# Sums of weight blocks made in DRAM by accumulating transfers, and loaded ready, in an encoder layer on one core

## Chip, cores and metric

The kernel runs on one core of a Trainium2 chip. The metric is the device time of one execution in microseconds. Three runs of the kernel before gave 1222.7, 1223.26 and 1224.56 us; the median is 1223.26 us.

## The reference

One layer of an encoder with 1024 tokens of width 1024, all in float32:

```python
h = rmsnorm(x, norm1_g) * (1.0 + sc1) + sh1
z = h @ w_in                                  # u, v, q, k, va, gate_a, gate_b
a_out = gmlp_branch(u, v, ...) @ w_a          # position mixing in chunks of 128, 8 groups
b_out = window_attention_branch(q, k, va, ...) @ w_b   # 8 heads, 2 kv heads, blocks of 128
merged = jax.nn.sigmoid(gate_a) * a_out + jax.nn.sigmoid(gate_b) * b_out
x = x + gt1 * (merged @ w_o)                  # w_o: 1024 x 1024

h2 = rmsnorm(x, norm2_g) * (1.0 + sc2) + sh2
f_gate, f_up = jnp.split(h2 @ w_ffn_in, 2, axis=-1)    # w_ffn_in: 1024 x 5632
x = x + gt2 * ((jax.nn.silu(f_gate) * f_up) @ w_ffn_out)
```

`sh1` to `gt2` come from a small conditioning product. The feed-forward has D_FF = 2816 hidden channels, 22 blocks of 128.

## The kernel before

**Products.** Each float32 operand is split into a high part (rounded by ScalarE) and a low part (the rest, by VectorE or GpSimd), and a product is three matmuls of 128x128 by 128x512. The gate products, the output projection and both feed-forward products are made by a scheme with seven block products in place of eight (Strassen's, in Winograd's form). It needs, besides blocks a11, a12, a21, a22 of a weight, sums and differences of them. In the kernel before, VectorE makes these sums from loaded weights: `merged_sums` (line 579) for w_o, in the attention stage of the second half of the tokens, with the result stored to the DRAM tile `sO`; `prep` (line 1812) for the gate and up weights of the feed-forward, block by block, into one tile `ws`, just before the split; `out_sums` (line 1911) for w_out, into the DRAM tile `wS`. The change touches the first two.

**Stages in order of time.** `half(0)` (line 643) handles the first 512 tokens: norm, the q/k product, the v product, eight attention steps (`for s in range(nw)`, line 1064), the spatial gating, the two branch projections. Then `half(1)` does the same for the other 512. `gate_products` (line 1385) makes the gate products for six column blocks d = 2 to 7, seven products each (i = 0 to 6). `out_products` (line 1489) is the output projection and the second norm. Then come 22 feed-forward blocks f, seven products each, and the second feed-forward product.

**An attention step.** At step s the scores of one block and kv head are made (`q_step`), the probabilities of the step before are transposed, exponentials are taken by ScalarE, `fill(FA)` and `fill(FB)` put three filler products (of u and of the gates) between them on TensorE, and `values` (line 552) multiplies by the values of the step before: ScalarE copies half of the result into a tile `xs` (a ring of two), VectorE adds, ScalarE makes the high part and GpSimd the low part (`mid<-xs,mid` in the profile). GpSimd also makes the low parts of filler weights (`prepare`, line 937; `wl<-raw,wh` on POOL) and the powers for the norms; after step 7 the one for `vr`, on which the spatial gating waits. In this stage the instructions of each compute engine are kept in program order.

**Queues.** Loads are issued by SyncE (SP), stores and a few loads by GpSimd, each in its own order. Weight units are loaded into a ring of three tiles `raw`; their high and low parts go to rings of three, `wh` and `wl`.

**Feed-forward order.** `order` (line 1991) lists the weight units (f, u), u = 1 to 3, in the order of preparation; `prepare(to, n)` (line 1998) makes up to n half preparations (high, then low) ahead of use. Unit 0 is the gate weight itself, units 1 and 2 are pairs of sums, unit 3 is a quarter of the up weight. In the kernel before, the gate weight of block f + 3 and the up weight of block f + 2 are loaded when units of block f are done.

Of the kernel before, what the change touches and what calls it, by code (L numbers as in the profile page):

```python
# [8 lines left out]
F32 = mybir.dt.float32  # L9
# [7 lines left out]
P = 128  # L17
# [90 lines left out]
def kernel(  # L108
# [58 lines left out]
    def nm(s):  # L167
        n_names[0] += 1
        return f"{s}_{n_names[0]}"
# [28 lines left out]
    def load(dst, src):  # L198
        ins = nc.sync.dma_start(dst, src)
        if not manual[0]:  # L200
            tc.keep_in_program_order(ins)

    def store(dst, src):
        nc.gpsimd.dma_start(dst, src)
# [112 lines left out]
    tA = dram.tile([NP, P, 4 * HALF], F32, tag="tA", name="tA")  # L317
    tB = dram.tile([NP, P, 4 * HALF], F32, tag="tB", name="tB")
    sO = dram.tile([KT // 2, P, 4 * HALF], F32, tag="sO", name="sO")


    apool_ctx = ExitStack()
# [66 lines left out]
    def ss_tile():  # L389
        return small.tile([P, 640], F32, tag="ss", name=nm("ss"), bufs=1)  # L390
# [182 lines left out]
    def open_ffn():  # L573
# [1 line left out]
        apool_ctx.close()  # L575
        fp = ffn_ctx.enter_context(pool("ffn"))
        fps.append(fp)

    def merged_sums(p):

        t = mid.tile([P, 2048], F32, tag="mid", name=nm("wo"))
        for i in range(2):
            load(t[:, i * UNIT : (i + 1) * UNIT], w_o[2 * p + i])
        a11, a12, a21, a22 = (t[:, i * HALF : (i + 1) * HALF] for i in range(4))
        ops = [(a22, a21, a22), (a21, a11, a21), (a11, a22, a11), (a12, a11, a12)]

        def one(n):
            out, a, b = ops[n]
            V.tensor_tensor(out, a, b, op=ALU.add)
            if n == 3:  # L590
                store(sO[p], t)
        return one

    halo_v = {}
    x1B = []
# [47 lines left out]
    def half(hf):  # L643
# [415 lines left out]
            V.tensor_copy(vgs[t], vps[t])  # L1059

        pts = None
        pair_sums = [merged_sums(0)] if hf else []
        adds = 0
        for s in range(nw):
            if s:
                prepare_due()
                sc = q_step(s)
                pts = transposed(st)
                den = exps(*sc, work[s][1])
            if hf == 0:  # L1070
                if s % 2 == 0:
                    ada_load()
                if s:
                    ada_late(*ada_loaded.pop(0), silu_c)
                if s == nw - 1:
                    ada_late(*ada_loaded.pop(0), silu_c)
            else:
                if s % 2 == 0 and s < nw - 2:
                    pair_sums.append(merged_sums(s // 2 + 1))
                for _ in range((0, 3, 3, 2, 2, 2, 2, 2)[s]):  # L1080
                    pair_sums[adds // 4](adds % 4)
                    adds += 1
            fill(FA)
            normalise(sc[0], sc[2], den)
            if s == 0:
                end_unit()
            st = sc[0]
            if s == nw - 1:
                for vg in vgs:
                    act[0] = after(A.activation(vg, vg, AF.Gelu_apprx_tanh), act[0])  # L1090
                for t, vg in enumerate(vgs[:3]):
                    V.tensor_tensor_reduce(
                        out=stream("hs"), in0=vg, in1=vg, op0=ALU.mult, op1=ALU.add,
                        scale=1.0, scalar=0.0, accum_out=vr[:, t : t + 1])
            if s:
                i, kv = work[s - 1]
                values(base + i, koff, kv, pts, vts, i, oH, oL)
            if s == nw - 1:
                A.activation(stream("hs"), vgs[3], AF.Square, accum_out=vr[:, 3:])
# [285 lines left out]
    def gate_products(hH, hL):  # L1385
# [21 lines left out]
        for d in GD:  # L1407
            banks = {}
            for i, (u, part, t, b, first) in enumerate(STEPS):
# [11 lines left out]
                elif i == 3:  # L1421
                    c22 = tmp()
                    A.copy(c22, bank)

                if i == 0:
                    gate_sums(d, 2)
                    gate_high(d, 2)
                elif i == 1:
                    gate_low(d, 2)
                elif i == 2:  # L1430
                    gate_high(d, 3)
                    merge(s, ps[1, 0])
                    gate_low(d, 3)
                elif i == 3:
                    gate_sums(d + 1, 1)
                elif i == 4:
                    gate_high(d + 1, 0)
                elif i == 5:
                    merge(c22, ps[0, 1])
                elif i == 6:  # L1440
                    gate_high(d + 1, 1)
                    merge(v, ps[0, 0])
                    V.tensor_tensor(merged[0][d // 4][:, d % 4, :], v, c22, op=ALU.add)
                    gate_low(d + 1, 1)
# [345 lines left out]
    T1, T2 = ((fpt(f"{n}h"), fpt(f"{n}l")) for n in ("tt1", "b22"))  # L1790


    RG, RU, U = {}, {}, {}
    a22 = []

    def gate_raw(f):
        r = wpool.tile([P, UNIT], F32, tag="raw", name=nm("raw"))
        dma(r, w_gate[f])
        return r

    def load_gate(f):
        if f < NF:
            RG[f] = gate_raw(f)
        else:
            fetch(f - NF)

    def load_up(f):
        if f < NF:
            RU[f] = ups[f % 2]
            dma(RU[f], w_up[f])  # L1810

    def prep(f, u, part):

        g, r = RG[f], RU.get(f)
        if part == 0:
            if u == 1:
                V.tensor_tensor(ws[:, Q:], r[:, :Q], r[:, Q:], op=ALU.add)
                V.scalar_tensor_tensor(out=ws[:, :Q], in0=ws[:, Q:], scalar=-1.0, in1=g[:, :Q],
                                       op0=ALU.mult, op1=ALU.subtract)
            elif u == 2:  # L1820
                V.tensor_tensor(ws[:, Q:], g[:, :Q], r[:, :Q], op=ALU.add)
                V.tensor_tensor(ws[:, :Q], g[:, Q:], ws[:, :Q], op=ALU.subtract)
            U[f, u] = wtiles(UNIT if u < 3 else Q)
            A.copy(U[f, u][0], (g, ws, ws, a22[0] if f == 0 else r[:, Q:])[u])
            return
        h, l = U[f, u]
        V.tensor_tensor(l, (g, ws, ws, a22[0] if f == 0 else r[:, Q:])[u], h.bitcast(F32), op=ALU.subtract)
        if u == 2:
            load_gate(f + 3)
        if u == 3 and f or (f, u) == (0, 2):  # L1830
            load_up(f + 2)

    BLK = {"B11": B11, "B21": B21, "T1": T1, "T2": T2}
    banks, keep, hidden = {}, {}, {}
# [94 lines left out]
    def low(src, t, k):  # L1929
        V.tensor_tensor(t[1][:, k, :], src, t[0][:, k, :].bitcast(F32), op=ALU.subtract)  # L1930
# [5 lines left out]
    def t2_sum(k):  # L1936
        V.scalar_tensor_tensor(out=X0[:, k, :], in0=X1[:, k, :], scalar=SHA(k + 4),
                               in1=X0[:, k, :], op0=ALU.add, op1=ALU.add)
        A.copy(T2[0][:, k, :], X0[:, k, :])

    def t34_sum(q, k):
        m = h2m[q][:, k, :]
# [12 lines left out]
    def chain_12(rb):  # L1955
        for k in range(4):
            chain.append(lambda k=k: scaled(X0, k, k, rb))
            chain.append(lambda k=k: t1_sum(k))
            chain.append(lambda k=k: scaled(X1, k, k + 4, rb))
            if k:  # L1960
                chain.append(lambda k=k: low(X0[:, k - 1, :], T2, k - 1))
            chain.append(lambda k=k: low(X0[:, k, :], T1, k))
            chain.append(lambda k=k: t2_sum(k))
        chain.append(lambda: low(X0[:, 3, :], T2, 3))

    def chain_rest():
        def new_block(name):
# [59 lines left out]
    def fetch(n):  # L2027
        if n < len(work):
            i, e = work[n]
            if outp:  # L2030
                r = outp[0].tile([P, UNIT], F32, tag="raw2", name=nm("raw2"))
            else:
                r = wpool.tile([P, UNIT], F32, tag="raw", name=nm("raw"))
            raws[n] = r
            dma(r[:, :Q], OUT[i][0](e))
            dma(r[:, Q:], OUT[i][1](e))
# [9 lines left out]

    with tc.manual_schedule():
        U[4, 0], U[5, 0], U[0, 0], U[1, 0] = early
        buf = mid.tile([P, 2048], F32, tag="mid", name=nm("ws"))
        ws, ups = buf[:, :UNIT], (buf[:, UNIT:], fp.tile([P, UNIT], F32, tag="ru", name="ru"))  # L2050
        load_up(0)
        load_up(1)
        g3 = gate_raw(3)
        load_gate(0)
        product(0, 0)
        U[2, 0] = wtiles()
        split2(raw2[0], *U[2, 0])
        evict(0, 0)
        load_gate(1)
        product(0, 1)  # L2060
        col_rstd(sums[1], NT, rcol[3])
        evict(0, 1)
        U[3, 0] = wtiles()
        split2(g3, *U[3, 0])
        load_gate(2)
        product(1, 0)
        rb = spread(rcol[3], NT)
        evict(1, 0)
        a22.append(ss_tile()[:, :Q])
        dma(a22[0], w_up[0][:, Q:])  # L2070
        prepare(0, 1)
        chain_12(rb)
        for f in range(1, EARLY):
# [246 lines left out]
```

## Time and profile before

| | |
|---|---|
| median of three runs | 1223.26 us (1222.7 to 1224.56) |
| profiled execution, its own time | 1221.94 us |
| its span, first to last instruction | 1220.2 us |
| granted TensorE clock, mean | 1.000 |
| TensorE (PE) busy | 1211.0 us, 99% of the span |
| VectorE (DVE) busy | 928.5 us, 76% |
| ScalarE (ACT) busy | 582.4 us, 48% |
| GpSimd (POOL) busy | 150.6 us, 12% |
| DMA packets | 236.54 MB, mean 194 GB/s |

A row of the timeline gives the start in us, the length in us, the engine and the operation with what it writes and reads; in brackets the engine's idle time before it and what ended that. A row of waits gives who waited, for whom, the total in us, the number of times and the longest. A row of a stretch gives its bounds, its length, busy times of PE, PEld (weight load), DVE, ACT and POOL, then the granted clock, the share of time in which the DMA engines were busy, and GB/s. L145 is the helper through which compute instructions are recorded, so the tiles tell them apart. DMA-issuing instructions are not counted as busy.

### The profile page before, as it was taken

What the parts mean: (1) busy time and instruction counts of PE and PEld (TensorE: products, weight loads), DVE (VectorE), ACT (ScalarE), POOL (GpSimd) and SP (SyncE); (2) the same over time, 40 slices, a digit from 0 to 9 for tenths busy, and PEclk for the clock granted to TensorE, in tenths of its full rate; (3) what the DMA queues carried; (4) which work ended last, traced back from release to release, by engine and by line L of the source; (5) the groups of instructions that cost most, each with busy time, mean ns of one, the idle gap of its engine ahead of it and who ended that gap; (6) DMA issues with size and microseconds to landing.
All of it is one profiled execution on the core that took longest, in us unless ns stands there. A gap on an engine that the chain in (4) does not pass through costs nothing.

```text
span 1220.2 us, 15626 instructions
## 1 busy us (share of the span) xinstructions
PE 1211.0 (99%) x5653; PEld 1007.2 (83%) x5653; DVE 928.5 (76%) x1504; ACT 582.4 (48%) x954; POOL 150.6 (12%) x182
## 2 busy tenths in 40 slices
PE   9999999999999999999999999999999999999998
PEld 7888888888888888877888888888888888888887
DVE  8999977789978776897997767675676766765646
ACT  5667865367855443644553333333333334433341
POOL 0024323024322000001100001000000000000001
PEclk9999999999999999999999999999999999999999
DMA  9752169653277233477313446455555449995552
GB/s 363 284 180 99 35 217 358 248 216 134 104 259 240 96 117 103 148 233 266 103 49 122 172 157 223 173 192 187 190 190 199 163 155 372 394 354 190 190 172 104
DMA packets 78096, 236.54 MB, mean 194 GB/s; under 512 B 8898, under 2 KB 9154, under 8 KB 72772
## 3 DMA queue, kind: packets, MB, share of 16 engines
q1 hardware_dynamic: 63028, 163.20, 38.6%
q0 software_dynamic: 14992, 72.36, 15.8%
q8 instruction: 44, 0.72, 0.3%
q14 instruction: 32, 0.26, 0.1%
HBM read 176.28 MB, written 59.24 MB: 193 GB/s over the span
## 4 chain that ended last, share of the span: by engine, by line
PE 93%; DVE 4%; issue 1%; DMA 1%; ACT 1%; POOL 0%; SPq 0%; DVEq 0%; ACTq 0%; POOLq 0%
PE mm L145 47%; PE at L145 46%; DVE mid L145 2%; DMA raw<-in_w_q_dram 1%; DVE wl L145 1%; DMA mid<-in_xA_dram 0%; DVE ss L145 0%; DVE h L145 0%; DVE ws L145 0%; ACT wh L145 0%; DVE t L145 0%; DVE tt1l L145 0%; ACT mid L145 0%; ACT h L145 0%; DVE b22l L145 0%
## 5 line engine op out<-in xcount | busy, mean ns | idle before, releaser
L145 DVE TENSOR_TENSOR wl<-raw,wh 128x1024 fp32r<-128x1024 f32 (+1 forms) x135 | 159.0, 1182 | 61.7 <-ACT wh L145 61.1
L145 ACT CAST wh<-raw 128x1024 fp32r<-128x1024 f32 (+1 forms) x149 | 152.2, 1023 | 112.1 <-PE mm L145 39.9
L145 PE MATMUL mm<-mid,wh 128*128 128x512 f32 x640 | 197.7, 390 | 0.8 <-DVE mid L145 0.8
L145 PEld LDWEIGHTS mm<-mid,wh 128*128 128x128 f32 x640 | 119.8, 188 | 25.8 <-DVE mid L145 1.2
L145 PE MATMUL mm<-wh,h 128*128 128x512 f32 x384 | 124.7, 397 | 0.5 <-ACT h L145 0.5
L145 PE MATMUL mm<-mid,wl 128*128 128x512 f32 x320 | 124.7, 390 | 0.0
L145 PE MATMUL mm<-h,wh 128*128 128x512 f32 x304 | 94.4, 392 | 0.0
L145 PE MATMUL at<-h,wh 128*128 128x512 f32 x304 | 93.9, 390 | 0.0
L145 PEld LDWEIGHTS mm<-wh,h 128*128 128x128 f32 x384 | 70.8, 188 | 14.2 <-ACT h L145 0.9
L145 DVE TENSOR_TENSOR wl<-ws,wh 128x1024 fp32r<-128x1024 f32 (+1 forms) x54 | 60.8, 1125 | 24.2 <-ACT wh L145 24.1
L145 ACT CAST wh<-ws 128x1024 fp32r<-128x1024 f32 (+1 forms) x54 | 52.5, 973 | 42.9 <-DVE ws L145 28.0
L145 PE MATMUL mm<-wl,h 128*128 128x512 f32 x192 | 71.2, 391 | 0.0
L145 PEld LDWEIGHTS mm<-mid,wl 128*128 128x128 f32 x320 | 60.1, 188 | 12.6
L145 PEld LDWEIGHTS at<-h,wh 128*128 128x128 f32 x304 | 56.9, 188 | 11.7
L145 PEld LDWEIGHTS mm<-h,wh 128*128 128x128 f32 x304 | 56.6, 188 | 11.6
L145 ACT ACTIVATE t<-t 128x512 f32<-128x512 f32 x46 | 28.4, 631 | 71.2 <-DVE t L145 71.2
L145 DVE TENSOR_TENSOR ol<-raw,oh 128x1024 fp32r<-128x1024 f32 x30 | 36.6, 1224 | 31.4 <-ACT oh L145 29.8
L145 PE MATMUL mm<-h,wl 128*128 128x512 f32 x152 | 59.4, 391 | 0.0
L145 PE MATMUL at<-h,wl 128*128 128x512 f32 x152 | 59.3, 390 | 0.0
L145 ACT ACTIVATE xs<-xs 128x512 f32<-128x512 f32 x21 | 13.3, 632 | 94.5 <-DVE xs L145 94.5
L145 ACT CAST oh<-raw 128x1024 fp32r<-128x1024 f32 x30 | 31.6, 1053 | 44.8 <-PE at L145 21.5
L145 PE MATMUL at<-wl,wh 128*128 128x512 f32 (+1 forms) x136 | 52.7, 388 | 0.0
(296 smaller groups left out, 2882.0 us busy)
## 6 DMA issues: line engine op xcount, KB each, us to landing
mid<-in_w_ada_dram SPq DMA_DIRECT2D x28, 512.0 KB, 8.3
raw<-in_w_gate_dram SPq DMA_DIRECT2D x28, 512.0 KB, 3.7
tA<-hid POOLq DMA_DIRECT2D x11, 1024.0 KB, 4.4
tB<-hid POOLq DMA_DIRECT2D x11, 1024.0 KB, 5.0
wo<-in_w_out_dram POOLq DMA_DIRECT2D x22, 512.0 KB, 5.9
wS<-wo POOLq DMA_DIRECT2D x11, 1024.0 KB, 5.2
raw<-wS SPq DMA_DIRECT2D x44, 256.0 KB, 3.4
raw<-tB SPq DMA_DIRECT2D x44, 256.0 KB, 5.2
```

The lines of the kernel that those rows point to most:

```text
L145: ins = f(*args, **kw)
```

## The change

The sums of w_o (all four pairs of blocks) and of the feed-forward's gate and up weights (all 22 blocks) are made in DRAM. For each group, four blocks of the weights are copied from DRAM to DRAM (to `sO`, or to a new DRAM tile `sF`) and four accumulating transfers add to them: two that need the copies, one that needs the first of these, one that needs the third. All are issued from GpSimd, each step behind a marker, a one-column copy on GpSimd that reads a tile of the compute stage, so that the step is issued at a chosen place. `plan_sums` gives the places: for w_o attention steps 0, 1, 3 and 5 of half 0; for feed-forward blocks 0 to 5 steps 1, 3, 5 and 7 of half 0; for blocks 6 to 11 steps 0, 2, 4 and 6 of half 1; for pairs of blocks from 12 to 21 products 0 and 4 of gate block d and of d + 1.

The feed-forward then loads units 1 and 2 ready from `sF` (two loads of 512 KB), and unit 3 as a quarter of the up weight (256 KB); each unit is loaded into a `raw` tile of its own, three units ahead. Two of the sums come with the opposite sign; the token block T2 is negated to match. `merged_sums` and the tiles of the sums on VectorE go.

```diff
+    sF = dram.tile([NF, P, 4 * HALF], F32, tag="sF", name="sF")
+
+    mark = [None]
+
+    def sum_dma(dst, src, **kw):
+        after(nc.gpsimd.dma_start(dst, src, **kw), mark[0])
+
+    def add_dma(dst, src):
+        sum_dma(dst, src, accum_op=ALU.add)
+
+    def sum_steps(dst, a11, a12, a21, a22):
+
+        S, w1, al, w2 = dst
+
+        def copies():
+            for d, a in zip(dst, (a11, a21, a12, a11)):
+                sum_dma(d, a)
+        return [copies, lambda: (add_dma(w1, a22), add_dma(w2, a21)), lambda: add_dma(S, w1),
+                lambda: add_dma(al, S)]
+
+    def quarters(t, f0, f1):
+        return [t[f0:f1, :, i * HALF : (i + 1) * HALF].rearrange("f p q -> p f q") for i in range(t.shape[2] // HALF)]
+
+    def ffn_sums(f0, f1):
+        return sum_steps(quarters(sF, f0, f1), *quarters(w_gate, f0, f1), *quarters(w_up, f0, f1))
+
+    def wo_sums():
+        w = [w_o.rearrange("(a b) p q -> b p a q", b=2)[i] for i in range(2)]
+        a = [w[i][:, :, j * HALF : (j + 1) * HALF] for i in range(2) for j in range(2)]
+        S, al, w2, w1 = quarters(sO, 0, KT // 2)
+        return sum_steps((S, w1, al, w2), *a)
+
+    sum_plan = {}
+
+    def plan_sums(steps, at):
+        for f, k in zip(steps, at):
+            sum_plan.setdefault(k, []).append(f)
+
+    def run_sums(ref, *k):
+        steps = sum_plan.pop(k, ())
+        if steps:
+            j = sm(8, "es")
+            mark[0] = G.tensor_copy(j[:, :1], ref)
+        for f in steps:
+            f()
+
+    plan_sums(wo_sums(), [(0, 0), (0, 1), (0, 3), (0, 5)])
+    plan_sums(ffn_sums(0, 6), [(0, 1), (0, 3), (0, 5), (0, 7)])
+    plan_sums(ffn_sums(6, 12), [(1, 0), (1, 2), (1, 4), (1, 6)])
+    for d in range(2, 7):
+        plan_sums(ffn_sums(8 + 2 * d, 10 + 2 * d), [(2, d, 0), (2, d, 4), (2, d + 1, 0), (2, d + 1, 4)])
...
-    def merged_sums(p):
...
@@ half(hf), attention steps
-            else:
-                if s % 2 == 0 and s < nw - 2:
-                    pair_sums.append(merged_sums(s // 2 + 1))
-                for _ in range((0, 3, 3, 2, 2, 2, 2, 2)[s]):
-                    pair_sums[adds // 4](adds % 4)
-                    adds += 1
+            run_sums(sc[1][:, :1], hf, s)
             fill(FA)
...
@@ gate_products
+                if i in (0, 4):
+                    run_sums((s if i == 0 else v)[:, :1], 2, d, i)
...
@@ feed-forward
+    def load_unit(n):
+        if n < len(order):
+            f, u = order[n]
+            if u == 0:
+                R[n] = gate_raw(f)
+            else:
+                R[n] = wpool.tile([P, UNIT], F32, tag="raw", name=nm("raw"))
+                if u < 3:
+                    dma(R[n], sF[f][:, (u - 1) * UNIT : u * UNIT])
+                else:
+                    dma(R[n][:, :Q], w_up[f][:, Q:])
         else:
-            fetch(f - NF)
+            fetch(n - len(order))
 
     def prep(f, u, part):
...
         if part == 0:
-            if u == 1:
-                V.tensor_tensor(ws[:, Q:], r[:, :Q], r[:, Q:], op=ALU.add)
-                V.scalar_tensor_tensor(out=ws[:, :Q], in0=ws[:, Q:], scalar=-1.0, in1=g[:, :Q],
-                                       op0=ALU.mult, op1=ALU.subtract)
-            elif u == 2:
-                V.tensor_tensor(ws[:, Q:], g[:, :Q], r[:, :Q], op=ALU.add)
-                V.tensor_tensor(ws[:, :Q], g[:, Q:], ws[:, :Q], op=ALU.subtract)
...
+            U[f, u] = wtiles(w.stop)
+            A.copy(U[f, u][0], R[n][:, w])
+        else:
+            split_low(R[n][:, w], *U[f, u])
+            load_unit(n + 3)
...
-        A.copy(T2[0][:, k, :], X0[:, k, :])
+        A.activation(T2[0][:, k, :], X0[:, k, :], AF.Identity, scale=-1.0)
+
+    def t2_low(k):
+        V.scalar_tensor_tensor(out=T2[1][:, k, :], in0=X0[:, k, :], scalar=-1.0,
+                               in1=T2[0][:, k, :].bitcast(F32), op0=ALU.mult, op1=ALU.subtract)
```

More of the change, by code (lines that the diff above doesn't have):

```diff
@@ L577, in open_ffn @@
         fps.append(fp)
-    def merged_sums(p):
[L581 to L592, printed above, removed]
     halo_v = {}
@@ L1061, in half @@
         pts = None
-        pair_sums = [merged_sums(0)] if hf else []
-        adds = 0
         for s in range(nw):
@@ L1790 @@
     T1, T2 = ((fpt(f"{n}h"), fpt(f"{n}l")) for n in ("tt1", "b22"))
-    RG, RU, U = {}, {}, {}
-    a22 = []
+    U, R = {}, {}
     def gate_raw(f):
@@ L1799, in gate_raw @@
         return r
-    def load_gate(f):
-        if f < NF:
-            RG[f] = gate_raw(f)
-        else:
-            fetch(f - NF)
[L1807 to L1810, printed above, removed]
+    def load_unit(n):
[9 more added lines that the diff above has]
+                    dma(R[n][:, :Q], w_up[f][:, Q:])
+        else:
+            fetch(n - len(order))
     def prep(f, u, part):
-        g, r = RG[f], RU.get(f)
+        n, w = place[f, u], slice(0, UNIT if u < 3 else Q)
         if part == 0:
-            if u == 1:
-                V.tensor_tensor(ws[:, Q:], r[:, :Q], r[:, Q:], op=ALU.add)
-                V.scalar_tensor_tensor(out=ws[:, :Q], in0=ws[:, Q:], scalar=-1.0, in1=g[:, :Q],
-                                       op0=ALU.mult, op1=ALU.subtract)
-            elif u == 2:
-                V.tensor_tensor(ws[:, Q:], g[:, :Q], r[:, :Q], op=ALU.add)
-                V.tensor_tensor(ws[:, :Q], g[:, Q:], ws[:, :Q], op=ALU.subtract)
[L1823 to L1831, printed above, removed]
+            U[f, u] = wtiles(w.stop)
[3 more added lines that the diff above has]
+            load_unit(n + 3)
     BLK = {"B11": B11, "B21": B21, "T1": T1, "T2": T2}
@@ L1960, in chain_12 @@
             if k:
-                chain.append(lambda k=k: low(X0[:, k - 1, :], T2, k - 1))
+                chain.append(lambda k=k: t2_low(k - 1))
             chain.append(lambda k=k: low(X0[:, k, :], T1, k))
             chain.append(lambda k=k: t2_sum(k))
-        chain.append(lambda: low(X0[:, 3, :], T2, 3))
+        chain.append(lambda: t2_low(3))
     def chain_rest():
@@ L2048 @@
         U[4, 0], U[5, 0], U[0, 0], U[1, 0] = early
[L2049 to L2052, printed above, removed]
         g3 = gate_raw(3)
-        load_gate(0)
+        load_unit(0)
         product(0, 0)
@@ L2058 @@
         evict(0, 0)
-        load_gate(1)
+        load_unit(1)
         product(0, 1)
@@ L2064 @@
         split2(g3, *U[3, 0])
-        load_gate(2)
+        load_unit(2)
         product(1, 0)
@@ L2068 @@
         evict(1, 0)
-        a22.append(ss_tile()[:, :Q])
-        dma(a22[0], w_up[0][:, Q:])
         prepare(0, 1)
```

## The prediction

> **What bounds the kernel now.** I read the page first, then the waits, then stretches of the timeline around the change.
>
> ```profile
> span 1220.2 us, 15626 instructions
> PE 1211.0 (99%) x5653; PEld 1007.2 (83%) x5653; DVE 928.5 (76%) x1504; ACT 582.4 (48%) x954; POOL 150.6 (12%) x182
> PE 93%; DVE 4%; issue 1%; DMA 1%; ACT 1%; POOL 0%; SPq 0%; DVEq 0%; ACTq 0%; POOLq 0%
> ```
>
> TensorE is busy for 1211.0 of 1220.2 us and carries 93% of the chain that ended last. All idle time of PE together is 9.2 us, a part of it at the start and the end, where this change does nothing. So work taken off VectorE pays only where PE stood waiting for VectorE, and everything else that the change does can only cost. The waits of PE and the stretches where VectorE is fullest say how much that is:
>
> ```profile
> PE mm L145 <- DVE mid L145: 0.8, 1, 0.8
> 263.00:295.00 32.00, 31.93 (x165) 26.46 (x164) 31.19 (x82) 21.86 (x57) 8.50 (x6) 1.00 0.43 158
> 598.00:617.00 19.00, 18.69 (x83) 15.18 (x83) 18.86 (x29) 9.75 (x16) 0.00 (x0) 1.00 0.21 79
> 264.60 0.16 DVE L145 TENSOR_TENSOR es<-rows,nmx 128x4 f32<-128x4 f32 x1
> 282.76 0.35 DVE L145 TENSOR_TENSOR es<-rows,nmx 128x4 f32<-128x4 f32 x1
> 291.54 0.55 DVE L145 TENSOR_TENSOR es<-rows,nmx 128x4 f32<-128x4 f32 x1
> 299.83 0.33 DVE L145 TENSOR_TENSOR es<-rows,nmx 128x4 f32<-128x4 f32 x1
> 316.42 0.35 DVE L145 TENSOR_TENSOR es<-rows,nmx 128x4 f32<-128x4 f32 x1
> ```
>
> A row of a stretch gives its length, then the busy time of PE, PEld, DVE, ACT and POOL, the granted clock, the DMA share and GB/s. In 263 to 295 us (attention steps of the second half, where the sums of w_o are made) VectorE is busy for 31.19 of 32 us. The `es` rows mark the steps: the fourth (282.76 to 291.54) takes 8.78 us, the next 8.29, so about 0.5 us is lost there. In 598 to 617 us (the feed-forward's first blocks) PE misses 0.31 us. The 0.8 us wait for `mid` is in the output projection, which keeps its VectorE work.
>
> **The sums on VectorE go.**
>
> ```profile
> L145 DVE TENSOR_TENSOR wo<-wo x60: 678/684/694, 274.2 to 1001.7; 128x512 f32<-128x512 f32 x60
> L145 DVE TENSOR_TENSOR ws<-raw,ws x33: 682/685/693, 607.0 to 990.5; 128x512 f32<-128x512 f32 x33
> ```
>
> 16 sums of w_o blocks (of the 60 `wo` rows; 44 are w_out's and stay) at 684 ns are 10.9 us; 22 x 4 sums of feed-forward blocks at 685 ns are 60.3 us. So 71 us leave VectorE, but PE gets back only the 0.5 + 0.3 = 0.8 us above. The sign change of T2 swaps operations of one shape for others: nothing. The loads and stores of w_o pairs go as well, 8.4 MB in the second half; the DMA shares that I use below still hold them.
>
> **The new loads of the feed-forward.**
>
> ```profile
> raw<-in_w_gate_dram SPq DMA_DIRECT2D x28, 512.0 KB, 3.7
> 391.37 2.72 PE at L145 x12
> ```
>
> A product of 12 matmuls takes 2.72 us (the chain's row), a block of seven 19 us. Per block f, 512 + 512 KB become 512 + 2 x 512 + 256 KB, 0.79 MB more, or 17.3 MB over 22 blocks, 419 us: 41 GB/s. A load lands in 3.7 us and is asked for three units ahead, about 14 us (four units in 19 us). I cost it at nothing; the cover is these 10 us of lead, and if it went, a load of 3.7 us would stand in front of a split once per unit. On SP's queue each load still waits only for its tile of three, as the gate weights' do now. The sums are first read near 600 us (the `ws` rows begin at 607.0) and are begun from 82 us on, so no load waits for a sum.
>
> **The transfers on GpSimd's queue.** Here is the cost. The diff issues copies and, behind them, additions that need the copies' landing. A DMA that needs another's landing holds GpSimd's queue, and the trace has this already:
>
> ```profile
> POOL wo L1257 <- DMA wS<-wo: 18.1, 4, 5.6
> L207 POOL DMA_DIRECT2D hd<-mid x1: 920/920/920, 48.9 to 48.9; - x1
> q0 software_dynamic: 14992, 72.36, 15.8%
> ```
>
> Behind the waiting addition stand GpSimd's own steps of the attention stage: the low parts of the outputs (`mid<-xs,mid`, 1.28 us), those of filler weights (`wl<-raw,wh`, 2.40) and the power of `vr`. Issuing one such DMA costs 0.92 us (512 rows), call it 1.
>
> Prices. GpSimd's queue moved 72.36 MB in 15.8% of 16 engines' 1220.2 us: 375 GB/s. A DRAM-to-DRAM transfer isn't in the trace. A copy costs between one move (375) and a load plus a store (188); I take one move, since the row counts a transfer's read and write once. An addition reads two blocks and writes one: between one move and three; I take two. So a w_o block set (1.05 MB) costs 2.8 us copied and 5.6 added, a set of six feed-forward blocks (1.57 MB) 4.2 and 8.4, times what other loads leave free:
>
> ```profile
> 82.00:106.00 24.00, 23.96 (x132) 20.27 (x131) 22.57 (x63) 16.34 (x44) 6.51 (x4) 1.00 0.45 161
> 106.00:122.00 16.00, 16.00 (x87) 13.78 (x86) 15.25 (x43) 11.88 (x30) 6.83 (x5) 1.00 0.20 67
> 122.00:146.00 24.00, 24.00 (x125) 19.98 (x124) 22.68 (x62) 20.16 (x48) 7.33 (x4) 1.00 0.15 45
> 81.90 0.16 DVE L145 TENSOR_TENSOR es<-rows,nmx 128x4 f32<-128x4 f32 x1
> 90.65 0.15 DVE L145 TENSOR_TENSOR es<-rows,nmx 128x4 f32<-128x4 f32 x1
> 106.32 0.55 DVE L145 TENSOR_TENSOR es<-rows,nmx 128x4 f32<-128x4 f32 x1
> 122.92 0.16 DVE L145 TENSOR_TENSOR es<-rows,nmx 128x4 f32<-128x4 f32 x1
> 111.12 1.28 POOL L145 TENSOR_TENSOR mid<-xs,mid 64x512 fp32r<-64x512 f32 x1 [4.27 <-ACT mid L145]
> 112.37 2.40 POOL L145 TENSOR_TENSOR wl<-raw,wh 128x1024 fp32r<-128x1024 f32 x1
> 125.67 0.59 ACT L145 COPY xs<-at 64x512 f32<-64x512 f32 x1
> 149.17 1.01 POOL L145 TENSOR_TENSOR vr<-vr,nhalf 128x4 f32<-128x4 f32 x1
> 154.65 1.21 DVE L145 TENSOR_TENSOR wl<-raw,wh 128x1024 fp32r<-128x1024 f32 x1
> 157.69 0.40 PE L145 MATMUL at<-mid,wh 128*128 128x256 f32 x2
> ```
>
> First half, by those rows. Step 0 (81.9): four w_o copies, 11.2 us at 55% free, land at 102. Step 1 (90.7): the w_o additions wait until 102; behind them 11.2 us of additions and 16.8 us of feed-forward copies, together 28.0: 2.1 by 106, 12.8 by 122, 13.1 at 85% free: 137.4. Step 3 (106.3): the feed-forward additions wait until 137.4. Two issues and the low part put the latter's end at 140.7 instead of 112.4. Its `xs` tile, one of two, is due again for ACT's copy at 125.67: PE loses 15.0 us, since VectorE and ACT stand behind that copy. Then 5.6 + 8.4 + 8.4 us of additions end at 144.0, 153.9 and 163.8. Step 5's sum waits for the second and issues at 154.9, its 8.4 us ending (behind w_o's last 5.6) at 180.3. Step 7's addition waits for that, and the power of `vr` starts at 182.6, due at 149.17 + 15.0 = 164.2; cover is 1.8 us (VectorE's last split ends at 155.86, PE needs it at 157.69): 16.6 lost. Half 0: 31.6 us. By one move per addition the same steps give 8.5 (all at the `xs` tile), by three 60, and 20 more in the second half.
>
> Second half: only feed-forward blocks 6 to 11.
>
> ```profile
> 295.00:311.00 16.00, 16.00 (x87) 13.79 (x86) 15.14 (x41) 13.07 (x33) 5.48 (x4) 1.00 0.26 98
> 311.00:327.00 16.00, 16.00 (x88) 13.38 (x87) 14.69 (x42) 12.88 (x32) 7.84 (x5) 1.00 0.31 113
> 302.51 0.58 ACT L145 COPY xs<-at 64x512 f32<-64x512 f32 x1 [1.05 <-PE at L145]
> 332.58 1.03 POOL L145 TENSOR_TENSOR vr<-vr,nhalf 128x4 f32<-128x4 f32 x1
> ```
>
> Copies: 16.8 us at 57% free from 264.6: 294. The wait of step 2 (282.76) ends there, the low part at 297.3, due at 302.51: nothing. The two additions end at 305.6 and 317.4, the third at 329.6; step 6 (316.42) waits for it, then four short steps, `vr` at 335.9 instead of 332.58: 1.5 us beyond the cover.
>
> Gate products, blocks 12 to 21:
>
> ```profile
> 407.69:483.85 76.16, 76.16 (x337) 63.09 (x337) 53.55 (x74) 30.99 (x45) 0.00 (x0) 1.00 0.33 105
> ```
>
> Each pair takes 5.6 + 11.2 us, five pairs 84 us at 67% free: 125 us from 391, done by 516. GpSimd has nothing else to do there (0.00 busy): no cost.
>
> Sum on the profiled execution's 1221.9 us: -0.8 + 31.6 + 1.5 = +32, 1254.2. The median shown is 1223.3, 1.3 above that execution: 1255.5, say 1256.
>
> **The rivals.** *Not slower: no waiting addition stands ahead of GpSimd's work.* If the waiting DMAs come out behind that work in its stream (the diff orders them only behind a marker), or land in time, the price is 0 and the gain 0.8: 1222.5. It decides at the low part of step 3: written before 125.67 or not. For it: the spacing of two steps (16.6 us) fits 6.3 MB at 375 GB/s on an idle queue. Against it: w_o has one step (9 us) for copies of 11.2, the loads take 15 to 45%, and the stage keeps GpSimd's steps in program order.
>
> *Far slower: a copy costs a load and a store, an addition three moves.* By the same steps at half and a third of 375 GB/s, step 1 waits until 117, step 3 until 177; the low part is 54 us late and `vr` 38 more; in the second half the copies land at 317, the low part 18 us late, `vr` 25 more: +135, 1357, and the lag could reach the output projection. The Trainium skill ("DMA: Bandwidth & Descriptors", "Latency and other measured facts") gives 207 to 214 GB/s for copies between HBM tensors; by it the 6.29 MB would take about 30 us instead of 16.8. No run here shows it. For this rival: both ends lie in one memory. Against: the one-move row is the only one of this queue.
>
> **How the numbers follow.** No blocking 0.24: 0.19 within 0.2% (2.4 us, about what the three runs, 1.9 us apart, can tell), and 0.05 faster, were VectorE's relief worth three times the 0.8. Forecast 0.46, with its own range from one move (1231) to three (1302) per addition. Far slower 0.30. The range goes from 1221 to 1320: some 0.04 lie below, some 0.15, the worse half of the far case, above. Slower: 0.76.
>
> **What would show it.** Right: GpSimd waits of 10 us and more for landings of the sums' transfers, ACT's `xs` copies late in steps 5 to 7, PE idle at 125 to 190 us, the second half nearly unhurt, VectorE 71 us emptier. Wrong: copies landing at other rates than 375 GB/s, PE busy through 80 to 160 us, or new waits for `raw` after 590 us.

## The result, and the profile after

The changed kernel takes 1260.68 us (median of 4 runs, 1259.23 to 1261.33) against 1222.98 for the kernel before in the same runs: a ratio of 1.031, 95% interval 1.0289 to 1.0326. The forecast was 1256 in 1221 to 1320. The profiled execution took 1260.43 us.

The page of the kernel after, the lines that answer to those of before (the last row is the granted TensorE clock in 40 slices):

```profile
span 1258.7 us, 15746 instructions
PE 1222.5 (97%) x5653; PEld 1016.3 (81%) x5653; DVE 877.1 (70%) x1400; ACT 579.0 (46%) x954; POOL 219.0 (17%) x263
PEclk9998879999999999999999999999999999999999
q0 software_dynamic: 35408, 122.70, 33.7%
PE 74%; DMA 16%; DVE 3%; issue 3%; ACT 2%; POOL 2%; SPq 0%; POOLq 0%; DVEq 0%; ACTq 0%
```

VectorE is 51 us emptier, not 71: the 104 sums are gone, but others of its instructions, most of them in half 0, take about 11 us longer (below). And busy time counts rows that overlap only once: the kernel of copies below, where nearly nothing is stretched, is 63 us emptier. PE still ends later: its idle time rises from 9.2 to 36.2 us, and its busy time by 11.5 us although it does the same 5653 matmuls. Transfers now carry 16% of the chain.

Both kernels have PE's matmuls in the same order, so the lag (the start of one and the same matmul, after minus before) tells where the time goes. In us, by stage, for the kernel after and for the experiments below (half 0 from 94 us on, ahead of the first hold):

| kernel | half 0 | half 1 | gate stage | output projection and first feed-forward blocks | rest |
|---|---|---|---|---|---|
| predicted | 31.6 | 1.5 | 0 | -0.8 (half 1's 0.5 included) | 0 |
| after | 28.2 | 0.4 | 12.5 | -2.6 | -0.4 |
| copies in place of additions | 0.3 | -1.3 | 1.8 | -2.7 | -0.4 |
| marker on its own column | 28.7 | 0.4 | 8.2 | -1.9 | -0.4 |
| holds without traffic | 19.0 | 0.0 | 1.0 | -0.4 | -0.2 |
| longer holds without traffic | 24.3 | -0.1 | 0.4 | 1.5 | 0.4 |
| other places, all blocks in DRAM | 1.0 | 1.1 | 0.8 | -2.7 | 24.3 |
| 6 blocks in DRAM | 1.0 | -1.2 | 0.7 | -2.4 | 2.3 |
| 12 blocks in DRAM | 0.7 | -1.3 | 0.2 | -2.3 | 1.2 |
| 16 blocks in DRAM | 0.9 | -1.2 | 11.4 | -2.7 | 1.2 |
| w_o early | 3.6 | -1.2 | 0.7 | -2.6 | 2.8 |
| needless addition at the scalings | 4.6 | 0.0 | 0.0 | 0.4 | -0.4 |
| the same behind the scalings | 0.0 | 0.0 | 0.7 | 1.1 | -0.5 |

Each row is one profiled execution. Where a kernel leaves a stage as it was, the lag still moves, by -0.4 to 1.5 us at the output projection.

Half 0 in the kernel after. First the timeline of GpSimd (brackets: idle time before, and what ended it), then the waits from 86 to 200 us (total, times, longest), then two stretches (PE, PEld, DVE, ACT, POOL busy, granted clock, DMA share, GB/s):

```profile
101.67 1.35 POOL L325 DMA_DIRECT2D sO<-in_w_o_dram  x1 [7.44 <-DMA sO<-in_w_o_dram]
136.84 1.38 POOL L325 DMA_DIRECT2D sF<-in_w_up_dram  x1 [9.11 <-DMA sF<-in_w_gate_dram]
137.68 1.83 POOL L145 TENSOR_TENSOR mid<-xs,mid 64x512 fp32r<-64x512 f32 x1
152.26 1.39 POOL L325 DMA_DIRECT2D sF<-sF  x1 [6.69 <-DMA sF<-in_w_up_dram]
175.12 1.38 POOL L325 DMA_DIRECT2D sF<-sF  x1 [12.06 <-DMA sF<-sF]
177.23 1.59 POOL L145 TENSOR_TENSOR vr<-vr,nhalf 128x4 f32<-128x4 f32 x1
...
PE at L145 <- DVE xs L145: 10.0, 2, 5.0
ACT mid L145 <- POOL vr L145: 8.0, 1, 8.0
ACT xs L145 <- POOL mid L145: 5.9, 1, 5.9
PE at L145 <- DVE lb L145: 5.0, 1, 5.0
...
90.00:120.00 30.00, 24.93 (x122) 20.88 (x122) 28.66 (x62) 17.48 (x44) 15.68 (x12) 0.91 1.06 316
120.00:150.00 30.00, 25.07 (x114) 21.31 (x113) 20.59 (x56) 17.88 (x45) 10.00 (x8) 0.86 1.07 276
```

The additions wait as forecast, and GpSimd's own steps stand behind them. But PE stops three times for about 5 us (near 112, 136 and 158 us) and once more behind `vr`, not twice; only one stop stands behind ScalarE's wait for the `xs` tile, the others behind VectorE. And the clock is granted at 0.86 to 0.91, where it was 1.00.

The gate stage, 420 to 550 us, the waits of the kernel after; behind them the landing of one group of loads from 440 to 545 us, first in the kernel before, then in the kernel after (last figure: median us from issue to landing):

```profile
DVE gsum L145 <- DMA raw<-in_w_gb_dram: 12.4, 4, 4.1
DVE t L145 <- POOL es L145: 8.3, 3, 4.5
DVE t L145 <- DMA xs<-pd: 6.7, 3, 2.6
PE mm L145 <- ACT t L145: 5.2, 2, 4.3
PE mm L145 <- DVE t L145: 3.6, 3, 1.6
...
raw<-in_w_gb_dram SPq DMA_DIRECT2D x2, 512.0 KB, 3.8
raw<-in_w_gb_dram SPq DMA_DIRECT2D x4, 512.0 KB, 10.1
```

Three new waits of VectorE stand here: for the marker (`es`, GpSimd's copy of a column of `s` or `v`, which VectorE then writes again), for gate weights that now land in 10.1 us, and for `xs` tiles loaded from the DRAM tile `pd` (256 KB each, stored there by the two halves). PE stops for 5.2 us behind ScalarE, which stands behind VectorE's wait for the marker, and for 3.6 us behind VectorE's `t`, which stands behind the loads. The forecast had none of them.

### The profile page after: what moved, and what is told of

It reads as the page before. It is cut to its first block, busy times and chain, and to the rows that moved or that the text cites. A ratio compares the mean times of both kernels' runs of the same rounds, so it can differ in the third digit from the quotient of the medians.

```text
span 1258.7 us, 15746 instructions
## 1 busy us (share of the span) xinstructions
PE 1222.5 (97%) x5653; PEld 1016.3 (81%) x5653; DVE 877.1 (70%) x1400; ACT 579.0 (46%) x954; POOL 219.0 (17%) x263
## 3 DMA queue, kind: packets, MB, share of 16 engines
q0 software_dynamic: 35408, 122.70, 33.7%
## 4 chain that ended last, share of the span: by engine, by line
PE 74%; DMA 16%; DVE 3%; issue 3%; ACT 2%; POOL 2%; SPq 0%; POOLq 0%; DVEq 0%; ACTq 0%
PE at L145 39%; PE mm L145 36%; DMA sF<-in_w_up_dram 8%; DMA sF<-sF 4%; DMA sO<-in_w_o_dram 1%; DVE mid L145 1%; DMA mid<-in_w_ada_dram 1%; POOL sF L325 1%; DMA raw<-in_w_q_dram 1%; DVE wl L145 1%; DMA raw<-in_w_ada_dram 1%; ACT mid L145 1%; DMA mid<-in_xA_dram 1%; ACT lb L145 0%; ACT wh L145 0%
## 5 line engine op out<-in xcount | busy, mean ns | idle before, releaser
L145 DVE TENSOR_TENSOR wl<-raw,wh 128x1024 fp32r<-128x1024 f32 (+1 forms) x201 | 227.8, 1136 | 129.6 <-ACT wh L145 128.9
L145 ACT CAST wh<-raw 128x1024 fp32r<-128x1024 f32 (+1 forms) x215 | 211.8, 987 | 113.3 <-PE at L145 38.3
L145 DVE TENSOR_TENSOR xs<-at,xs 128x512 f32<-128x512 f32 (+1 forms) x44 | 30.3, 689 | 37.9 <-PE at L145 30.5
L145 PE MATMUL at<-wh 128*128 128x512 f32 (+1 forms) x136 | 52.7, 387 | 0.0
L145 PE MATMUL at<-wh,wl 128*128 128x512 f32 (+1 forms) x136 | 52.7, 387 | 0.0
```

What stands on the lines that cost most here:

```text
L145: ins = f(*args, **kw)
```

## The experiments

**Traffic without holds.** Every transfer stays at its place with its size, but all eight are plain copies that wait for nothing.

```diff
-        return [copies, lambda: (add_dma(w1, a22), add_dma(w2, a21)), lambda: add_dma(S, w1),
-                lambda: add_dma(al, S)]
+        return [copies, lambda: (sum_dma(xw1, a22), sum_dma(xw2, a21)), lambda: sum_dma(xS, a21),
+                lambda: sum_dma(xal, a11)]
```

> All eight transfers of each group are issued at their old places, but as plain copies of input blocks to DRAM blocks of their own: same number of transfers and same sizes, no addition, no transfer that needs another's landing. The sums are left out, so the feed-forward and the output projection read other numbers. Theory (GpSimd's queue is held by additions that wait; what stands behind them is late): the lag against the kernel before at the end of half 0 falls from 28.4 us to 3 or less, the lag of the gate stage from 12.4 to 2 or less, the whole time is 1219 to 1229 us. Rival (the transfers' traffic itself slows loads and engines): copies move 2 bytes where additions move 3, so about three quarters of the traffic stays, and three quarters of the loss: 1247 to 1253 us. Rival (the traffic lowers TensorE's granted clock): granted clock stays near 0.9 from 90 to 180 us although PE does not stand idle, +8 to +12 us.

Measured: 1218.75 us, ratio 0.997 (0.9957 to 0.9983). One stretch of half 0, and the software queue's row:

```profile
120.00:150.00 30.00, 30.00 (x154) 24.88 (x153) 28.78 (x75) 25.39 (x59) 13.97 (x13) 1.00 1.02 343
q0 software_dynamic: 28752, 122.70, 29.1%
```

The DMA engines are full (1.02) here too, PE is busy without a gap, and the clock stays at 1.00. Both rivals fall for half 0. The row also prices the transfers: from 15.8% of 1220.2 us to 29.1% of 1216.9 is 161 us of all 16 engines, to 33.7% of 1258.7 is 231; with 11 us for the stores of w_o that went, 172 us for 54.5 MB as copies (317 GB/s) and 242 us where half of them are additions. So an addition costs (242 - 86) / 86 = 1.8 copies, by an estimate that takes copies to cost the same in both kernels.

**Holds without traffic.** The kernel before, with chains of tiny additions (2 KB) in half 0, each waiting for the one before.

```diff
+    HOLD = {0: 0, 1: 4, 3: 10, 5: 3, 7: 5}
...
+            for i in range(HOLD[s]):
+                after(nc.gpsimd.dma_start(hb[i % 2], hb[1 - i % 2], accum_op=ALU.add), m)
```

> The kernel before, with its sums on VectorE, and in half 0 at the same places chains of tiny accumulating transfers (2 KB each, 4, 10, 3 and 5 of them at steps 1, 3, 5 and 7), each needing the landing of the one before, so that GpSimd's queue is held for about 9, 22, 7 and 11 us while nearly no bytes move. Theory (holding alone): PE idles at the same steps, lag at the end of half 0 of 18 to 30 us, the whole time 1241 to 1253 us, and the granted clock falls to about 0.9 behind the idle stretches. Rival (traffic): lag of 3 us or less, 1223 to 1226 us, granted clock 1.0.

Measured: 1240.6 us, ratio 1.0141 (1.0124 to 1.0158). As these holds ended earlier than the sums' (step 1's low part starts at 100.07 us, in the kernel after at 105.89), a second run had longer chains: `HOLD = {0: 0, 1: 6, 3: 9, 5: 4, 7: 6}`.

> The kernel before with the chains of tiny additions made 6, 9, 4 and 6 long at steps 1, 3, 5 and 7, so that each holds GpSimd about as long as the sums do in the changed kernel (about 15, 22, 8 and 14 us from the marker on). Theory (holds and the catching up behind them are all of half 0's loss): lag at the end of half 0 of 24 to 31 us, 1246 to 1254 us. Rival (the transfers' traffic adds the 9 us by which the shorter chains fell short): lag of 22 us or less, 1240 to 1245 us.

Measured: 1246.4 us, ratio 1.0194 (1.0178 to 1.021). One stretch of the second kernel:

```profile
120.00:150.00 30.00, 25.79 (x126) 22.10 (x125) 21.25 (x60) 18.10 (x43) 15.36 (x17) 0.89 0.08 19
```

With 8% of the DMA engines in use, half 0 loses 24.3 us, and the clock falls to 0.89. So holds alone give about 24 of the 28.2 us, and the low clock goes with PE's idling, not with traffic. Of the other 4 us nothing more is known: from the marker to the low part behind it, these holds are 1.2 and 1.3 us shorter than the sums' at steps 1 and 3, and 0.5 and 1.2 us longer at steps 5 and 7.

**One hold, and what follows it.** Only w_o's additions wait, at the changed kernel's places; the first 6 feed-forward blocks are summed in half 1 and the others on VectorE. The kernel with 6 blocks (below) differs from it in one line:

```diff
-    plan_sums(wo_sums(), [(0, 0), (0, 3), (0, 5), (0, 7)])
+    plan_sums(wo_sums(), [(0, 0), (0, 1), (0, 3), (0, 5)])
```

> As the kernel with 6 blocks, but w_o's steps at 0, 1, 3 and 5 of half 0, the places of the changed kernel: its first additions wait for the copies' landing in front of step 1's low part. Theory: one hold of 9 to 11 us, PE loses 3 to 7 us near 100 to 115 us and nothing after, so 1222 to 1228 us. Rival (half 0 loses only where the feed-forward's additions queue behind w_o's): as the kernel with 6 blocks, within 1 us.

Measured: 1226.24 us, ratio 1.0025 (1.0016 to 1.0034); the kernel with 6 blocks 1221.53. PE stops once, for 2.5 us at 111 us. The timeline there:

```profile
107.45 1.12 DVE L145 TENSOR_TENSOR den<-den,es 128x4 f32<-128x4 f32 x1
108.41 0.58 ACT L145 COPY xs<-at 64x512 f32<-64x512 f32 x1 [0.99 <-PE at L145]
108.63 2.39 POOL L145 TENSOR_TENSOR wl<-raw,wh 128x1024 fp32r<-128x1024 f32 x1
108.82 3.82 DVE L145 TENSOR_SCALAR lb<-lb,den 128x384 f32<-128x384 f32 x4
112.56 0.67 DVE L145 TENSOR_TENSOR xs<-at,xs 64x512 f32<-64x512 f32 x1
```

ScalarE's copy into `xs` waits for PE, not for GpSimd: the ring of two covers this hold. What is late is VectorE. Its four scalings `lb` take 3.82 us where the kernel before needs 1.41, and a sum of 128x4 takes 1.12 instead of 0.16, while GpSimd works off what the hold had put back.

**Is it GpSimd's work that stretches VectorE's?** The kernel before, with one needless addition (128x512) on GpSimd in steps 1 to 6 of half 0: once started with the scalings, once behind them.

```diff
+            if hf == 0 and 1 <= s <= 6:       # first kernel: ahead of normalise
...
+                extra(sc[2])
             normalise(sc[0], sc[2], den)
+            if hf == 0 and 1 <= s <= 6:       # second kernel: behind it
...
+                extra(sc[0][3])
```

> The kernel before, with one needless addition (128x512) on GpSimd in each of steps 1 to 6 of half 0, started when the exponentials' extra column is ready, so that it runs while VectorE does den and the four scalings lb. Theory (VectorE's small sums and its scalings stand while a GpSimd instruction runs, so GpSimd's catching up after a hold costs PE a second time): den or the scalings take 0.8 to 1.5 us longer in these steps, and VectorE has no room for it: 2 to 8 us in all, 1225 to 1231 us. Rival (GpSimd's work has no effect on VectorE, only late low parts cost): 1222 to 1224 us.

> The control: the same addition in the same steps, started behind the scalings, when VectorE goes on with the sum of the outputs and the maxima. Theory: those instructions are not held, at most the next low parts shift a little: 1222.5 to 1225 us. Rival (any more work on GpSimd at these steps costs the same): as with the addition at the scalings.

Measured: 1227.56 us, ratio 1.0046 (1.0034 to 1.0059), and 1222.53, ratio 0.9998 (0.9989 to 1.0006). One step of the first kernel, and behind it the same step of the second:

```profile
108.95 1.29 POOL L145 TENSOR_TENSOR hs<-t,t 128x512 f32<-128x512 f32 x1
109.19 2.26 DVE L145 TENSOR_SCALAR lb<-lb,den 128x384 f32<-128x384 f32 x4
...
108.25 1.41 DVE L145 TENSOR_SCALAR lb<-lb,den 128x384 f32<-128x384 f32 x4
109.86 1.30 POOL L145 TENSOR_TENSOR hs<-t,t 128x512 f32<-128x512 f32 x1
```

The scalings take 0.75 to 0.86 us longer for a GpSimd instruction that runs beside them, in each of these six steps, and half 0 loses 4.6 us. The same instruction 0.9 us later costs nothing. So the place counts, not the amount. The Trainium skill ("SBUF — State Buffer", "Who interferes with whom") has a cause for it: VectorE and GpSimd share a pair of ports; an operation like VectorE's scalings can take that pair, and whichever engine issues first then keeps the other out for its whole instruction. The rows agree: the addition starts 0.24 us ahead of the scalings, and 1.41 us become 2.26.

**The gate stage: the marker.** It reads a column of its own, which ScalarE copies.

```diff
-                    run_sums((s if i == 0 else v)[:, :1], 2, d, i)
...
+                    A.copy(z, (s if i == 0 else v)[:, :1])
+                    run_sums(z, 2, d, i)
```

> In the gate stage the marker reads a one-column tile of its own, copied by ScalarE, instead of a column of the tile s or v that VectorE writes again; all transfers stay. Theory (the marker stands behind waiting additions on GpSimd and so holds s and v; VectorE's sum into that tile waits for it, ScalarE and PE behind VectorE): the 12.4 us of the gate stage go, the lag there is 2 us or less, the whole time 1247 to 1251 us. Rival (the transfers fill the DMA engines from 420 to 540 us, and loads of gate weights come late): no change, 1258 to 1262 us. Half 0 is as in the changed kernel under both: 28 us.

Measured: 1257.26 us, ratio 1.0279 (1.0263 to 1.0294). 4 of the 12 us go, not 12: the theory holds for a third, and the rival for the rest. The two overlap: without the marker's wait PE's 5.2 us behind ScalarE are gone, but its stops behind VectorE's `t` grow from 3.6 to 5.6 us.

**The gate stage: the loads.** Three kernels with the marker on its own column, w_o at steps 0, 3, 5, 7 of half 0 and blocks 0 to 5 at steps 0, 3, 5, 7 of half 1. Blocks below FD are summed in DRAM, the others on VectorE as before: none, three or five pairs of blocks in the gate stage.

```diff
+            elif f >= FD:
+                if u == 1:
+                    RU[f] = ups[f % 2]
+                    dma(RU[f], w_up[f])
...
+    plan_sums(wo_sums(), [(0, 0), (0, 3), (0, 5), (0, 7)])
+    plan_sums(ffn_sums(0, 6), [(1, 0), (1, 3), (1, 5), (1, 7)])
+    for d in (2, 4, 6):                       # FD = 12; none for FD = 6; for 16: range(2, 7), 2 + 2 * d
+        plan_sums(ffn_sums(4 + d, 6 + d), [(2, d, 0), (2, d, 4), (2, d + 1, 0), (2, d + 1, 4)])
```

> In DRAM only the sums of w_o (steps 0, 3, 5, 7 of half 0) and of feed-forward blocks 0 to 5 (steps 0, 3, 5, 7 of half 1); blocks 6 to 21 are summed by VectorE as in the kernel before; nothing in the gate stage. Theory (holds cost, and loads that come late behind full DMA engines; the sums of the first blocks are where VectorE's relief pays): no hold in half 0, 1 us or less in half 1, nothing in the gate stage, and the gains of 2.5 to 4 us seen where sums had left VectorE: 1218 to 1222 us. Rival (the relief is worth 0.8 us at most, as forecast): 1222 to 1225 us.

> As the kernel with 6 blocks, and blocks 6 to 11 also in DRAM, in three pairs in the gate stage with the marker on its own column. Theory: the gate stage loses 0.5 to 1.5 us (DMA engines at 0.8, loads a little later), 1218.5 to 1223 us. Rival (the gate stage's loss is of the marker alone): as the kernel with 6 blocks, within 0.5 us.

> As the kernel with 6 blocks, and blocks 6 to 15 also in DRAM, in five pairs in the gate stage at the places of the changed kernel, with the marker on its own column. Theory (full DMA engines: the gate weights' loads take 10 us instead of 3.8, and VectorE's sums of gate weights wait for them): the gate stage loses 6 to 10 us, 1225 to 1231 us, of which none is a wait for the marker. Rival (the 8 us that stayed with the marker's own column came from what half 0 and half 1 had left queued): 2 us or less, 1219 to 1224 us.

Measured: 1221.53 us, ratio 0.9985 (0.9976 to 0.9994); 1220.34, 0.9977 (0.9966 to 0.9987); 1230.78, 1.0062 (1.0049 to 1.0076). The stretch from 450 to 480 us with 12 and with 16 blocks, the gate weights' landing from 425 to 520 us with 12 and with 16, and two waits with 16; then the landing of `pd` loads with 16, and, for the kernel of copies, the landing of both and its wait for gate weights (425 to 560 us):

```profile
450.00:480.00 30.00, 30.00 (x134) 24.86 (x133) 20.02 (x27) 12.52 (x21) 6.92 (x10) 1.00 0.79 217
450.00:480.00 30.00, 28.55 (x126) 23.30 (x126) 16.61 (x24) 12.10 (x20) 9.10 (x12) 1.00 1.03 267
raw<-in_w_gb_dram SPq DMA_DIRECT2D x3, 512.0 KB, 4.7
raw<-in_w_gb_dram SPq DMA_DIRECT2D x3, 512.0 KB, 9.8
DVE t L145 <- DMA xs<-pd: 13.0, 4, 4.9
DVE gsum L145 <- DMA raw<-in_w_gb_dram: 10.4, 3, 3.5
xs<-pd SPq DMA_DIRECT2D x8, 256.0 KB, 9.2
...
raw<-in_w_gb_dram SPq DMA_DIRECT2D x3, 512.0 KB, 9.0
xs<-pd SPq DMA_DIRECT2D x8, 256.0 KB, 5.8
DVE gsum L145 <- DMA raw<-in_w_gb_dram: 10.0, 3, 3.8
```

Three pairs leave the DMA engines at 0.79, the loads land in 4.7 us, and the stage loses 0.2, less than expected. Five pairs fill them (1.03), the same loads take 9.8 us, and the stage loses 11.4, a little more than expected, with nothing left over from earlier stages and no wait for the marker. In VectorE's queue the sums that free PE's banks stand behind instructions that wait for these loads. Late gate weights alone do not make the loss: in the kernel of copies they land in 9.0 us and VectorE waits for them as long (10.0 us), and the stage loses 1.8. What it has not is the wait for `pd`: those loads land in 5.8 us there, in 9.2 with 16 blocks, and PE's two longer stops with 16 blocks (3.72 us until 486 and 2.17 until 509) each stand behind a wait of 4.9 us for them. The engines are at 0.98 from 450 to 480 us in the kernel of copies and at 0.71 from 480 to 510. Whether that last bit of share or the additions themselves make the `pd` loads late was not tried, and no kernel with four pairs was run.

The kernel with 12 blocks is 0.23% faster than the kernel before. It keeps what the change gains and pays nothing for it up to the first feed-forward blocks; 1.2 us go later, in the feed-forward, where VectorE once waits 4.5 us for the landing of a store.

**The same bytes elsewhere.** All sums in DRAM: w_o in half 0 at steps 0, 3, 5 and 7, blocks 0 to 5 in half 1, 6 to 11 in the gate stage, 12 to 21 in the feed-forward itself.

```diff
+    for f in range(2, 12, 2):
+        plan_sums(ffn_sums(10 + f, 12 + f), [(3, f, 1), (3, f, 3), (3, f + 1, 1), (3, f + 1, 3)])
```

> The same sums and the same bytes at other places: w_o at steps 0, 3, 5 and 7 of half 0; feed-forward blocks 0 to 5 in half 1; blocks 6 to 11 in three pairs in the gate stage with the marker on its own column; blocks 12 to 21 in five pairs in feed-forward blocks 2 to 11. Theory (what costs is an addition that waits in front of GpSimd work that is due): w_o's copies have 24 us instead of 9, so half 0 loses 2 us or less, half 1 about 1, the gate stage 1 or less, and the 2.8 us that the changed kernel gains behind the gate stage stay: 1219 to 1226 us. Rival (the traffic costs wherever it lies): 1245 to 1262 us.

Measured: 1245.38 us, ratio 1.018 (1.0165 to 1.0195): the number is at the rival's edge, but the place is not the rival's. Up to the first feed-forward blocks, with about 60% of the bytes moved (w_o and 12 of 22 blocks), the lag is -0.4 us; then 24.3 us are lost. Waits from 690 to 900 us, the stretch from 760 to 800, and the landing of a hidden block's store from 690 to 840 us, with that of the kernel after, over its whole execution, behind it:

```profile
DVE wo L145 <- issue: 14.8, 2, 11.6
DVE hid L145 <- DMA tB<-hid: 15.9, 3, 12.2
DVE hid L145 <- DMA wS<-wo: 11.6, 1, 11.6
PE mm L145 <- DVE wl L145: 6.8, 1, 6.8
760.00:800.00 40.00, 35.38 (x148) 28.46 (x147) 19.50 (x26) 10.38 (x17) 10.89 (x16) 0.96 1.04 313
tB<-hid POOLq DMA_DIRECT2D x4, 1024.0 KB, 12.6
...
tB<-hid POOLq DMA_DIRECT2D x11, 1024.0 KB, 5.2
```

The transfers that wait are the same; what stands behind them is another thing, the stores of the feed-forward. They are issued late, behind waiting additions, and land late in full DMA engines (12.6 us instead of 5.2). VectorE waits 12.2 and 11.6 us to write tiles again whose stores haven't landed, and PE stops behind it for 4.0 us (at 784 us) and 6.8 (at 817). A third stop, 6.2 us at 731, stands behind VectorE's sums of w_out (`wo`), which wait 11.6 us; the view names no one for this wait, and the likeliest is their loads, which share GpSimd's queue. How much is of late issue and how much of late landing was not told apart.

## Why the prediction was right, and where not

**The bound and the price: right.** The holds came where they were expected: w_o's additions waited until 101.67 us (forecast 102), the feed-forward's until 136.84 (137.4), the third until 152.26 (154.9), the last until 175.12 (180.3). One move for a copy and two for an addition gave these; measured are 317 GB/s and 1.8 copies. The rival with copies of two moves and additions of three had 117 and 177 for the first two. The Trainium skill's 207 to 214 GB/s for copies ("DMA: Bandwidth & Descriptors", "Latency and other measured facts") is for transfers issued from other queues; it lies near that rival, and the measured 317 does not.

**Half 0: 31.6 forecast, 28.2 measured, by other terms.** The step that failed is "PE loses 15.0 us" at the `xs` tile, with the holds of steps 1 and 5 at nothing. Each of the first three holds cost 7 to 8 us, 22 in all: step 3's by the `xs` tile, the others by VectorE, which stands while GpSimd catches up. For step 1 the run with one hold shows this, and the needless additions show how; for step 5 the rows alone do (two operations of 128x4, `es` and `mod`, took 2.56 and 2.17 us beside GpSimd). Behind step 3's hold the lag was 15.2 us, as forecast, but half of it had been lost at step 1: the transfers set when that hold ends, whatever was lost before. The term at `vr` was sized 16.6 and measured 6.3: `vr` started at 177.23 instead of 182.6, and it was due some 7 us later, because the lag ahead of it was 22 and not 15. So the two errors nearly cancel: what is lost earlier need not be lost again at the last hold. That they cancel so closely is luck.

**The clock: not in the forecast.** 11.5 us of the loss are PE's busy time. Behind a stop of some microseconds the matmuls run at half rate, as these rows of the kernel after show, from the gate stage and from a later stretch without gaps:

```profile
534.47 1.20 PE L145 MATMUL mm<-mid,wh 128*128 128x512 f32 x2 [4.27 <-ACT t L145]
535.89 1.05 PE L145 MATMUL mm<-mid,wh 128*128 128x512 f32 x2
536.75 0.63 PE L145 MATMUL mm<-mid,wl 128*128 128x512 f32 x1
...
559.98 0.62 PE L145 MATMUL mm<-h,wh 128*128 128x512 f32 x2
560.43 0.39 PE L145 MATMUL mm<-h,wl 128*128 128x512 f32 x1
```

Two matmuls take 0.86 us from start to start behind the idle 4.27 us (535.89 to 536.75) and 0.45 later. The Trainium skill ("TensorE: Matmul & The Clock Gate", "Part 1: The HAM clock gate") has the clock halved after an idle window of some 3.4 us, until PE has been busy as long. These rows agree. In the kernel after, the lag grows by some 2.1 us more within 7 us behind each of the three 5-us stops, by 3.6 around the short stops at `vr`, and by 1.7 behind this one. Stops of 0.8 to 1.6 us in its gate stage left the clock at 1.00. But a shorter stop than 3.4 us was enough once: behind one of 2.80 us (marker on its own column) the granted clock was 0.72 over the next 6 us, behind one of 2.54 us (w_o early) 1.00.

**Half 1: 1.5 forecast.** The stage lost 0.4, and those kernels in which no addition waits there for more than 2 us gained 1.2: so the hold cost 1.6. That the sizes agree is luck. The forecast had the loss at `vr`, which started in time (362.02, 29.4 behind the kernel before, at a lag of 29.2); PE's one stop, 1.2 us at 325 us, stands behind VectorE, whose `den` took 2.25 us instead of 0.16 while GpSimd caught up after a wait of 5.3 us.

**The gate stage: 0 forecast, 12.5 measured.** This is the step that was wrong: "GpSimd has nothing else to do there: no cost". The forecast asked who stands behind the addition on GpSimd's queue and overlooked the marker, which holds a tile of VectorE's (4 us), and it used the free share of the DMA engines for the transfers without asking what full engines do to the loads that share them, of gate weights and of `pd` (8 to 11 us).

**VectorE's relief: 0.8 forecast, 3.8 measured** (1.2 in half 1, 2.6 at the output projection and the first feed-forward blocks). Two waits of PE in the kernel before, in the second norm that follows the output projection, are part of it:

```profile
PE at L145 <- POOL rcol L145: 1.2, 1, 1.2
PE at L145 <- DVE ss L145: 0.3, 1, 0.3
```

GpSimd's power for `rcol` stands behind VectorE. In the kernel after PE has no wait for `rcol`; the forecast showed only the wait for `mid`. Every kernel with w_o and the first 6 blocks in DRAM has it; which of the two gives it was not tried.

**The rivals.** "No waiting" would have needed the low part of step 3 before 125.67 us; it came at 137.68. "Far slower" fell with the price.

The total came out near by luck, because errors cancel: 12.5 us missing in the gate stage stand against 3.4 too many in half 0, 1.1 in half 1 and 2.2 of gain behind the gate stage that was not forecast (3.0 against 0.8). That leaves the 5.8 between 32.3 forecast and 38.1 in the table.

## What to carry to other kernels

A transfer that must wait for another's landing should stand on a compute engine's queue only where nothing due stands behind it: that includes the marker that places it, stores whose tiles are written again, and the burst of work afterwards, which can slow a neighbour. Give each step the time of its transfers at the free share of the DMA engines, and keep that share below full: at 0.79 the gate weights landed in 4.7 us, at 1.03 in 9.8. One late load may be hidden (1.8 us in the kernel of copies); two kinds of them in one queue were not (11.4). A stop of PE of 3 us or more is paid a second time by its clock; the short stops of the gate stage were not.

## What the runs showed of the hardware

- GpSimd's instruction stretches some of VectorE's that run beside it: four scalings 128x384 from 1.41 to 3.82 us, a sum of 128x4 from 0.16 to 1.12. The sums that read `at` (PSUM) beside GpSimd work were not stretched: `pL<-at,pH` takes 0.68 us (median) in half 0 of the kernel before and of the kernel after.
- In a chain of tiny additions in DRAM (2 KB each), each waiting for the landing of the one before, two issues on GpSimd stand 2.31 us apart (97.24 and 99.55 us); the first link took 5.4 us (from 89.39 to 94.83 us).
- Full DMA engines alone (1.02) cost half 0 at most 0.3 us, in the kernel of copies.
